# Layer 0's experts: TensorE's products in one fixed order, quarter-array products in two blocks an expert

## The chip, the cores and the metric

The kernel runs on one core of one Trainium2 chip. The metric is the device time of one execution in microseconds (us); the time before is 2729.64 us, the median of 3 runs (2728.22 to 2730.44). One execution under the profiler took 2732.13 us, with a span of 2730.4 us from its first to its last recorded instruction. TensorE multiplies (PE), VectorE and ScalarE (DVE, ACT) do the elementwise work, GpSimd (POOL) adds and issues the indirect transfers, SyncE (SP) issues the others.

## The reference

A block of two layers works on 1024 latent rows and 256 context rows of width 1024, in fp32. In each layer three token mixers (neighbourhood attention, a gated linear recurrence, a short convolution) are followed by 16 experts with expert choice: each expert takes its best rows, 128 latent rows and, in layer 0 alone, 32 context rows. Cut to what the change touches:

```python
def _expert_choice_ffn(h, w_router, w_gate, w_up, w_down):
    cap = EC_CAPACITY_FACTOR * t // N_EXPERTS          # 128 of 1024 latent rows, 32 of 256 context rows
    vals, idx = lax.top_k(aff.transpose(0, 2, 1), cap)
    xg = jax.vmap(lambda hb, ib: hb[ib])(h, idx)
    hid = silu(einsum('becd,edf->becf', xg, w_gate)) * einsum('becd,edf->becf', xg, w_up)
    out = einsum('becf,efd->becd', hid, w_down) * vals[..., None]
    return zeros.at[ib.reshape(-1)].add(ob.reshape(-1, d))

x  = x  + m_lat[5] * _expert_choice_ffn(h2,  w_router[l], w_exp_gate[l], w_exp_up[l], w_exp_down[l])
if need_ctx:                                           # layer 0 only
    cx = cx + m_ctx[5] * _expert_choice_ffn(hc2, w_router[l], w_exp_gate[l], w_exp_up[l], w_exp_down[l])
```

`w_exp_gate` and `w_exp_up` are 1024 x 512 per expert, `w_exp_down` is 512 x 1024.

## The kernel before, in words

`experts` (called once per layer) runs over the 16 experts. For each it does the following; the line is that of the code before.

- **Rows and weights.** `slots` turns the expert's column of ranks into row numbers with two small bf16 products per row tile (`slp`, L1148; the operand `O` is made on VectorE, L1144). `gather` (L1165) fetches 128 latent rows (`xg`) and the context's rows as quarters of a row (`xgc`) by indirect DMAs on GpSimd. `expert_w` (L1218) loads the weights as six tiles of 1 MB (`est`, two halves each of gate, up and down) on SyncE.
- **Transposing the rows** (`expert_x`). `xg` is transposed on TensorE in two halves of four 128 x 128 transposes (`xt`, L1231). Both halves go to the same PSUM bank, number 4 (`bank("xt")`, one buffer). For each half VectorE multiplies (`xm`, L1233, the only reader of the bank), GpSimd adds (L1234), ScalarE casts the high part (`xh`, L1235) and VectorE takes the rest (`xo`, L1236). The context's two transposes (`xtc`, L1244) go to bank 7, which the `slp` products share.
- **Gate and up** (`expert_up`). `split` makes of each weight half a high and a low part (`ewh` on ScalarE, L1178; `ewl` on VectorE, L1182) in three buffers. Per half 12 products (`pg`, L1280: high by high, rest by high, high by low) of the full array are accumulated over 128 latent rows. The context's products (`pgc`, L1265) take the fp32 weights as they are and use a quarter of the array's columns each (32 of 128), four side by side, into bank 5; four follow each weight half. `sc` copies them out.
- **The hidden layer** (`expert_hid`). `hid` (L1296, L1297) is transposed (`hidp`, L1300, bank 4) and copied (`hidT`, L1302). For the context four products sum the quarters (`hcp`, L1309, quarter array, bank 6); `hidc` and `upc` (L1312 to L1314) follow, two transposes on 64 rows (`hct`, L1317, bank 6), and `hcT` (L1319).
- **Down** (`expert_down`). Eight fp32 products for the latents (`pd`, L1335, banks 2 and 3) and eight on a quarter of the array for the context (`pdc`, L1341, bank 6), then `yo`, `yd`, `yc` (L1346 to L1352) and two indirect DMAs that add rows to the results (L1170).

Behind the last expert the modulation of layer 1 is computed (`adaln`: `aps`, L157, and `atp`, L171), the rows are loaded and normalised again, and the first projection of layer 1 (`pj`, L288) begins.

Within an engine the order of instructions is chosen by a scheduler from its own estimates of times; `issue_after` is the means by which the code can tie one instruction behind another. Before, TensorE's instructions of the experts have no such tie among themselves, and those of several steps lie among each other: an `xt` half stands between gate products, quarter-array groups stand between all others.

A plain fp32 product leaves two records in the trace: the eight `pd` of an expert are 16 records, and a group of four `pgc` is eight.

```python
ps = self.bank("xt" if need else "xt2", [P, 4, P], F32, "xt")      # need: layer 0; bank 4 alone
for j in range(4):
    nc.tensor.transpose(ps[:, j], xg[:, (k + j) * P:(k + j + 1) * P], self.idf)
xm = ep.tile([P, 4, P], F32, name="xm", bufs=2)
nc.vector.tensor_tensor(xm, ps, ...)
```

Of the kernel before, what the change touches and what calls it, by code (L numbers as in the profile page):

```python
# [19 lines left out]
P = 128  # L20
# [22 lines left out]
class Kern:  # L43
# [1177 lines left out]
    def expert_x(self, l, r, ep, eng=None):  # L1221
# [16 lines left out]
        if need:  # L1238
# [4 lines left out]
            for c in range(2):  # L1243
                nc.tensor.transpose(ps[:, c], xgc[:, c * P:(c + 1) * P], self.idf)  # L1244
# [5 lines left out]

    def expert_up(self, l, r, ep, first=False):
# [4 lines left out]
        pc, sc = None, []  # L1256

        def ctx_mm(gu, hf, st):

            nonlocal pc  # L1260
            if hf == 0:
                pc = self.bank("upc", [P, 512], F32, "pgc")
            for k in range(4):
                kk = 4 * hf + k
                nc.tensor.matmul(pc[32 * k:32 * k + 32], r["xc"][:, kk % 2, 32 * (kk // 2):32 * (kk // 2) + 32],  # L1265
                                 st[:, 512 * k:512 * k + 512], start=hf == 0, stop=hf == 1, tile_position=(0, 32 * k),
                                 skip_group_check=True)
            if hf == 1:
                t = ep.tile([P, 512], F32, name=f"sc{gu}", bufs=1)
                nc.scalar.copy(t, pc)  # L1270
                sc.append(t)
        late = []
        for gu in range(2):
            n = 0
            for hf in range(2):
                st = r[("gate", "up")[gu]][hf]
                wh, wl = r["pre"].pop(0) if r.get("pre") else self.split(self.ws, st, [P, 2048], "ew", 3)
# [5 lines left out]
                if need:  # L1283
                    late.append((gu, hf, st))
                    if len(late) > 1 * first:
                        ctx_mm(*late.pop(0))
        for x in late:
            ctx_mm(*x)
        return acc, sc

    def expert_hid(self, l, r, up, ep):
        nc = self.nc
        need = l < DEPTH - 1
        (pg, pu), sc = up
        hid = ep.tile([P, 512], F32, name="hid", bufs=1 + need)
        nc.scalar.activation(hid, pg, AF.Silu)  # L1296
        nc.vector.tensor_tensor(hid, hid, pu, ALU.mult)  # L1297
        ps = self.bank("xt" if need else "downc", [P, 4, P], F32, "hidp")
        for j in range(4):
            nc.tensor.transpose(ps[:, j], hid[:, j * P:(j + 1) * P], self.idf)  # L1300
        hT = ep.tile([P, 4, P], F32, name="hidT", bufs=2)
        nc.scalar.copy(hT, ps)  # L1302
        if need:

            ps = self.bank("downc", [P, 256], F32, "hcp")
# [5 lines left out]
            hc, uc = [ep.tile([64, 256], F32, name=n, bufs=1) for n in ("hidc", "upc")]  # L1311
            nc.scalar.activation(hc, ps[:64], AF.Silu)  # L1312
            nc.vector.tensor_copy(uc, ps[64:])
            nc.vector.tensor_tensor(hc, hc, uc, ALU.mult)  # L1314
            ps = self.bank("downc", [P, 2, 64], F32, "hct")
            for c in range(2):
                nc.tensor.transpose(ps[:, c], hc[:, P * c:P * c + P], self.idf[:64, :64])  # L1317
            hcT = ep.tile([P, 2, 2, 32], F32, name="hcT", bufs=2)
            nc.vector.tensor_copy(hcT.rearrange("p h c s -> p c h s"), ps.rearrange("p c (h s) -> p c h s", h=2))  # L1319
        return hT, (hcT if need else None)  # L1320

    def expert_down(self, l, r, hid, ep, g5, g5c, xl, xc):
# [6 lines left out]
        for hf in range(2):  # L1329
            st = r["down"][hf]  # L1330

            for k in range(2):
                for nn in range(2):
                    c = 1024 * k + 512 * nn
                    self.downed = nc.tensor.matmul(po[nn], hT[:, 2 * hf + k], st[:, c:c + 512],  # L1335
                                                   start=hf == 0 and k == 0, stop=hf == 1 and k == 1)
            for k in range(2):
                if need:
                    for nn in range(2):
                        o = 64 * k + 32 * nn  # L1340
                        nc.tensor.matmul(pd[o:o + 32], hcT[:, hf, k], st[:, 1024 * k + 512 * nn:1024 * k + 512 * nn + 512],  # L1341
                                         start=hf == 0, stop=hf == 1, tile_position=(0, o), skip_group_check=True)
# [12 lines left out]
    def experts(self, l, xl, xc):  # L1355

        nc = self.nc
        with self.pool(f"ex{l}") as ep, self.pool(f"ws{l}") as self.ws, self.pool(f"ew3_{l}") as ew3:
# [12 lines left out]
            self.nw = 0  # L1371

# [18 lines left out]
            start(2, rs[0]["xd"])  # L1391
            for e in range(NE):
# [146 lines left out]
```

## Time and profile before

| | |
|---|---|
| median of 3 runs | 2729.64 us (2728.22 to 2730.44) |
| profiled execution | 2732.13 us |
| its span | 2730.4 us, 55190 instructions |
| PE busy | 2504.4 us (92%) |
| DVE busy | 1884.3 us (69%) |
| ACT busy | 1131.4 us (41%) |
| POOL busy | 669.3 us (25%) |
| chain that ended last | PE 67%, DVE 18%, DMA 5%, issue 4%, ACT 3% |
| in it: `pg` / `pd` / `pgc` | 13% / 8% / 2% |
| DMA | 507.12 MB, mean 186 GB/s |

The profiled execution lies 2.5 us above the median and 1.7 us above its span. A busy share is a mean over the whole program, whose stages differ: layer 0's experts lie between about 1005 and 1458 us, and what bounds them must be read there, not from the shares. The chain is followed backwards from the last instruction to whatever released each one; a step that stands in it was late there in this execution.

### The profile page before, as it was taken

The numbers are of one execution on the slowest core, as the hardware profiler recorded it, in microseconds if no ns is written. First come the engines' busy times: TensorE is split into PE (matmuls) and PEld (weight loads), VectorE is DVE, ScalarE is ACT, GpSimd is POOL, SyncE is SP. The second block draws the span as 40 slices with busy tenths as digits, with TensorE's granted clock in tenths as the row PEclk, the third lists the DMA queues.
The fourth block names the chain that finished last, engine by engine and source line by source line (L and its number), as shares of the span: only waits on it lengthen the run. The fifth ranks groups of instructions, "written<-read, shape, count | busy, mean of one in ns | idle before, by whom it ended". The sixth has DMA issues, their size and how long they took to land.

```text
span 2730.4 us, 55190 instructions
## 1 busy us (share of the span) xinstructions
PE 2504.4 (92%) x21959; PEld 1906.9 (70%) x21959; DVE 1884.3 (69%) x4046; ACT 1131.4 (41%) x1878; POOL 669.3 (25%) x621
## 2 busy tenths in 40 slices
PE   7999999998999979999996999999958899589997
PEld 4998887894677855555554988778844677367664
DVE  4258887857666586777754368787858874787874
ACT  4224433324554534444434334333314554345452
POOL 1000000035444633333311000000045532222241
PEclk9999999998999979999998999999979999789999
DMA  7332324247354948888887332423176355889994
GB/s 281 102 108 71 114 68 123 66 138 243 113 160 135 349 151 278 281 280 279 283 280 212 94 105 74 124 84 89 49 200 225 94 163 183 300 281 370 377 376 127
DMA packets 347936, 507.12 MB, mean 186 GB/s; under 512 B 53380, under 2 KB 203072, under 8 KB 346592
## 3 DMA queue, kind: packets, MB, share of 16 engines
q1 hardware_dynamic: 336416, 465.85, 50.4%
q0 software_dynamic: 11264, 37.75, 5.9%
q8 instruction: 173, 2.83, 0.4%
q14 instruction: 83, 0.68, 0.1%
HBM read 410.10 MB, written 94.90 MB: 185 GB/s over the span
## 4 chain that ended last, share of the span: by engine, by line
PE 67%; DVE 18%; DMA 5%; issue 4%; ACT 3%; POOL 2%; SPq 1%; POOLq 0%; DVEq 0%; ACTq 0%
PE pg L1280 13%; PE pj L277 12%; PE pd L1335 8%; PE pj L288 8%; PE po L828 6%; PE nao L786 3%; PE pgc L1265 2%; PE npt L762 2%; PE sA L733 1%; DVE Kt L375 1%; PE aps L157 1%; DVE Kt L376 1%; DVE Qt L378 1%; PE hl L365 1%; PE xt L1231 1%
## 5 line engine op out<-in xcount | busy, mean ns | idle before, releaser
L1182 DVE TENSOR_TENSOR ewl<-est,ewh 128x2048 fp32r<-128x2048 f32 x126 | 298.1, 2371 | 109.7 <-ACT ewh L1178 108.6
L1178 ACT CAST ewh<-est 128x2048 fp32r<-128x2048 f32 x128 | 243.4, 1905 | 170.9 <-PE pg L1280 130.5
L277 PE MATMUL pj<-hl,whi 128*128 128x320 f32 (+2 forms) x912 | 310.2, 340 | 0.0
L277 PE MATMUL pj<-hh,whi 128*128 128x320 f32 (+2 forms) x912 | 309.9, 340 | 0.0
L277 PE MATMUL pj<-hh,wlo 128*128 128x320 f32 (+2 forms) x912 | 308.7, 339 | 0.0
L288 PE MATMUL pj<-whi,hh 128*128 128x256 f32 x960 | 277.8, 290 | 4.5 <-ACT nev L566 4.1
L288 PE MATMUL pj<-whi,hl 128*128 128x256 f32 x960 | 276.8, 291 | 0.8 <-DVE hl L239 0.8
L288 PE MATMUL pj<-wlo,hh 128*128 128x256 f32 x960 | 275.5, 288 | 0.0
L1335 PE MATMUL pd<-est,hidT 128*128 128x512 f32 x512 | 232.2, 596 | 2.1 <-ACT hidT L1302 2.1
L288 PEld LDWEIGHTS pj<-whi,hh 128*128 128x128 f32 x960 | 186.0, 194 | 8.8 <-ACT nev L566 5.2
L288 PEld LDWEIGHTS pj<-wlo,hh 128*128 128x128 f32 x960 | 185.9, 194 | 2.2 <-issue 1.3
L288 PEld LDWEIGHTS pj<-whi,hl 128*128 128x128 f32 x960 | 184.6, 194 | 3.5 <-issue 1.3
L277 PEld LDWEIGHTS pj<-hh,whi 128*128 128x128 f32 x912 | 172.2, 189 | 13.7 <-issue 0.9
L277 PEld LDWEIGHTS pj<-hl,whi 128*128 128x128 f32 x912 | 172.2, 189 | 13.5 <-issue 1.9
L277 PEld LDWEIGHTS pj<-hh,wlo 128*128 128x128 f32 x912 | 172.1, 189 | 13.0 <-issue 1.1
L1335 PEld LDWEIGHTS pd<-est,hidT 128*128 128x128 f32 x512 | 95.2, 189 | 110.7 <-issue 103.3
L265 DVE TENSOR_TENSOR wlo<-wst,whi 128x1024 fp32r<-128x1024 f32 (+1 forms) x72 | 75.2, 1058 | 131.7 <-ACT whi L264 130.6
L1280 PE MATMUL pg<-ewh,xh 128*128 128x512 f32 x512 | 156.8, 424 | 3.1 <-ACT xh L1235 3.0
L752 POOL TENSOR_SCALAR S<-S,sm 128x768 f32<-128x768 f32 (+2 forms) x108 | 108.6, 1007 | 188.3 <-DVE sm L751 166.8
L1280 PE MATMUL pg<-ewl,xh 128*128 128x512 f32 x512 | 147.7, 404 | 0.0
L1280 PE MATMUL pg<-ewh,xo 128*128 128x512 f32 x512 | 142.3, 398 | 2.1 <-DVE xo L1236 2.1
L750 ACT ACTIVATE S<-S,mn 128x768 f32<-128x768 f32 (+2 forms) x108 | 98.6, 913 | 85.2 <-DVE mn L745 79.6
(369 smaller groups left out, 5560.9 us busy)
## 6 DMA issues: line engine op xcount, KB each, us to landing
est<-in_w_exp_gate_dram SPq DMA_DIRECT2D x64, 1024.0 KB
est<-in_w_exp_up_dram SPq DMA_DIRECT2D x64, 1024.0 KB
est<-in_w_exp_down_dram SPq DMA_DIRECT2D x64, 1024.0 KB
wm<-in_w_mod_dram SPq DMA_DIRECT2D x80, 512.0 KB
wst<-in_w_in_dram SPq DMA_DIRECT2D x88, 256.0 KB
pna<-nev SPq DMA_DIRECT2D x180, 64.0 KB
wos<-in_w_out_dram SPq DMA_DIRECT2D x42, 256.0 KB
mst<-mix SPq DMA_DIRECT2D x32, 320.0 KB
```

The costliest lines, as they stand in the source:

```text
L265: nc.vector.tensor_tensor(b, c, a, ALU.subtract)
L277: nc.tensor.matmul(ps[:, :cn], sel(a(k)), b[:, k, c0:c0 + cn], start=n == 0, stop=n == 3 * KD - 1)
L288: nc.tensor.matmul(ps[:, :2 * P], b[:, k, t * P:(t + 1) * P], a(k).rearrange("p a n -> p (a n)"), start=n == 0, stop=n == 3 * KD - 1)
L750: nc.scalar.activation(S[:, :w], S[:, :w], AF.Exp, scale=-1.0, bias=mn[:, 1:2], accum_out=sm[:, 0:1])
L752: nc.gpsimd.tensor_scalar(S[:, :w], S[:, :w], sm[:, 1:2], 1.0, ALU.mult, ALU.mult)
L762: nc.tensor.transpose(pt[:kn, i], S[:, c:c + kn], self.idf)
L786: nc.tensor.matmul(po[64 * X:64 * X + 64, gi], V[:kn, tt, 64 * X:64 * X + 64], PT[X][:kn, i], start=i == 0, stop=i == len(ch) - 1, tile_po ...
L828: nc.tensor.matmul(ps, a, b, start=n == 0, stop=n == len(ops) - 1)
L1178: nc.scalar.copy(hi, src)
L1182: nc.vector.tensor_tensor(lo[:, :m], src[:, :m], hi[:, :m], ALU.subtract)
L1280: nc.tensor.matmul(acc[gu], a[:, 4 * hf + k], b[:, 512 * k:512 * k + 512], start=n == 0, stop=n == 3 * KD - 1)
L1335: self.downed = nc.tensor.matmul(po[nn], hT[:, 2 * hf + k], st[:, c:c + 512], start=hf == 0 and k == 0, stop=hf == 1 and k == 1)
```

## The change

All of it concerns the experts of layer 0 (`need`); layer 1 keeps its order.

- A new helper `then` ties each TensorE product or transpose inside it behind the one before it (`self.pel`). In layer 0 all of `expert_x`, `expert_up`, `expert_hid`, `expert_ctx`, `expert_ctx_hid` and `expert_down` runs under it, so that their order on TensorE is that of the code. The `slp` products of `slots` stay untied.
- The context's gate and up products (`ctx_mm`) are put together: 16 in a row between the latent's gate and up products (behind both for the first expert), into banks 5 and 6.
- `hcp` moves directly behind the up products and ahead of `pdc` of the expert before it, so that these two also form one block. `hcp` and `hct` use bank 5 in place of 6.
- `hct` transposes 128 rows of `hidc` (64 of them filled before; now `hidc` has 128 rows and ScalarE fills all), and `hcT` reads the first 64 columns.
- `expert_x` of the expert after next is called between `pdc` and `pd` (`mid`), both of its halves directly behind each other.

```diff
         for k in range(0, KD, 4):
             ps = self.bank("xt" if need else "xt2", [P, 4, P], F32, "xt")
             for j in range(4):
-                nc.tensor.transpose(ps[:, j], xg[:, (k + j) * P:(k + j + 1) * P], self.idf)
+                with self.then(need):
+                    nc.tensor.transpose(ps[:, j], xg[:, (k + j) * P:(k + j + 1) * P], self.idf)
...
+    def then(self, on=True):
...
+        def after(f):
+            def g(*a, **k):
+                with tc.issue_after(self.pel.ins) if self.pel is not None else nullcontext():
+                    self.pel = f(*a, **k)
+                return self.pel
+            return g
+        nc.tensor.matmul, nc.tensor.transpose = after(mm), after(tr)
...
+        with self.then(need):
+            prods(0)
+            if need and not first:
+                ctx_mm(0)
+                ctx_mm(1)
+            prods(1)
+            if need and first:
+                ctx_mm(0)
+                ctx_mm(1)
         return acc, sc
...
+    def expert_ctx(self, sc):
+
+        nc = self.nc
+        ps = self.bank("upc", [P, 256], F32, "hcp")
+        with self.then():
             for i, t in enumerate(sc):
                 for h in range(2):
                     o = 64 * i + 32 * h
                     nc.tensor.matmul(ps[o:o + 32], self.sel, t[:, 256 * h:256 * h + 256], start=True, stop=True,
                                      tile_position=(0, o), skip_group_check=True)
...
+        hc, uc = ep.tile([P, 256], F32, name="hidc", bufs=1), ep.tile([64, 256], F32, name="upc", bufs=1)
+        nc.scalar.activation(hc, ps, AF.Silu)
+        nc.vector.tensor_copy(uc, ps[64:])
+        nc.vector.tensor_tensor(hc[:64], hc[:64], uc, ALU.mult)
+        pt = self.bank("upc", [P, 2, P], F32, "hct")
+        with self.then():
             for c in range(2):
-                nc.tensor.transpose(ps[:, c], hc[:, P * c:P * c + P], self.idf[:64, :64])
...
+                nc.tensor.transpose(pt[:, c], hc[:, P * c:P * c + P], self.idf)
...
         if need:
             pd = self.bank("downc", [P, 512], F32, "pdc")
+            with self.then():
...
+            if mid:
+                mid()
         po = [self.bank("down", [P, 512], F32, "pd") for _ in range(2)]
...
             for e in range(NE):
                 if e + 3 <= NE:
                     start(e + 3, rs[e + 1]["xd"])
-                hid = self.expert_hid(l, rs[e], up, ep)
-                if e + 2 < NE:
+                if not need and e + 2 < NE:
                     self.expert_x(l, rs[e + 2], self.xp)
                 if e + 1 < NE:
                     up = self.expert_up(l, rs[e + 1], ep)
-                self.expert_down(l, rs[e], hid, ep, g5, g5c, xl, xc)
+                    if need:
+                        pc = self.expert_ctx(up[1])
+                more = lambda: self.expert_x(l, rs[e + 2], self.xp) if e + 2 < NE else None
+                self.expert_down(l, rs[e], (hid, hidc if need else None), ep, g5, g5c, xl, xc, more)
+                if e + 1 < NE:
+                    hid = self.expert_hid(l, rs[e + 1], up, ep)
+                    if need:
+                        hidc = self.expert_ctx_hid(pc, ep)
```

How this moves the instructions is shown for TensorE and VectorE. A row is the line, the operation, the result and its operands, the tile's shape and how many follow each other; after the change every tied TensorE instruction has the line of the helper's caller (L1265).

TensorE in a middle expert before, from a quarter-array group among the gate products on:

```order
L1231 MATMUL xt<-idf,xg 128x128 x3
L1309 MATMUL hcp<-sc_13529,sel 32x256 x2
L1309 MATMUL hcp<-sc_13572,sel 32x256 x2
L1231 MATMUL xt<-idf,xg 128x128
L1244 MATMUL xtc<-idf,xgc 128x128 x2
L1280 MATMUL pg<-ewl,xh 128x512 x3
L1280 MATMUL pg<-ewh,xh 128x512 x4
L1280 MATMUL pg<-ewh,xo 128x512 x4
L1280 MATMUL pg<-ewl,xh 128x512 x4
L1335 MATMUL pd<-est,hidT 128x512 x5
L1265 MATMUL pgc<-est,xct 32x512 x8
L1335 MATMUL pd<-est,hidT 128x512 x3
```

After the change, the block of context products of one expert:

```order
L1265 MATMUL pgc<-est,xct 32x512 x5
L1148 LDWEIGHTS O
L1148 MATMUL slp<-pay,O 128x5
L1148 LDWEIGHTS O
L1148 MATMUL slp<-pay,O 128x5
L1265 MATMUL pgc<-est,xct 32x512 x11
```

The two `slp` rows stand inside the block, which is so in 12 of the 16 experts. From the last up products on to the next expert's gate products:

```order
L1265 MATMUL pg<-ewl,xh 128x512 x4
L1265 MATMUL hcp<-sc_13929,sel 32x256 x2
L1265 MATMUL hcp<-sc_13940,sel 32x256 x2
L1265 MATMUL pdc<-est,hcT 32x512 x8
L1265 MATMUL xt<-idf,xg 128x128 x8
L1265 MATMUL xtc<-idf,xgc 128x128 x2
L1265 MATMUL pd<-est,hidT 128x512 x8
L1265 MATMUL hidp<-idf,hid 128x128 x4
L1265 MATMUL hct<-idf,hidc 128x128 x2
```

Here the two halves of `xt`, formerly between gate and up products, stand directly behind each other and behind `pdc`, and the quarter-array instructions stand in one block of `pgc` and one of `hcp` with `pdc`.

VectorE in a middle expert before, around the two `xm` that read the halves:

```order
L1233 TENSOR_TENSOR xm<-xt,A_12256 128x512
L1351 TENSOR_TENSOR yd<-pdc,yd 64x512
L1352 SCALAR_TENSOR_TENSOR yc<-yd,val,g5c 64x512
L1160 TENSOR_REDUCE val<-slp 128x1
L1182 TENSOR_TENSOR ewl<-est,ewh 128x2048
L1236 TENSOR_TENSOR xo<-xm,xh 128x512
L1233 TENSOR_TENSOR xm<-xt,A_12256 128x512
L1247 TENSOR_TENSOR xct<-xtc,A_12256 128x256
L1182 TENSOR_TENSOR ewl<-est,ewh 128x2048
L1248 TENSOR_TENSOR xct<-xct,mt_93 128x256
L1313 COPY upc<-hcp 64x256
```

After the change:

```order
L1182 TENSOR_TENSOR ewl<-est,ewh 128x2048
L1349 TENSOR_TENSOR hid<-hid,pg 128x512
L1182 TENSOR_TENSOR ewl<-est,ewh 128x2048
L1333 COPY upc<-hcp 64x256
L1234 TENSOR_TENSOR xm<-xt,A_12256 128x512
L1391 TENSOR_TENSOR yd<-pdc,yd 64x512
L1334 TENSOR_TENSOR hidc<-hidc,upc 64x256
L1392 SCALAR_TENSOR_TENSOR yc<-yd,val,g5c 64x512
L1234 TENSOR_TENSOR xm<-xt,A_12256 128x512
L1249 TENSOR_TENSOR xct<-xtc,A_12256 128x256
L1237 TENSOR_TENSOR xo<-xm,xh 128x512
```

Now `hid`, an `ewl` (of the following expert's first up half) and `upc` stand ahead of the first `xm`, and three small instructions on the context between the two `xm`.

TensorE at the start of layer 0's experts before, behind the first expert's own transposes:

```order
L1231 MATMUL xt<-idf,xg 128x128 x8
L1148 LDWEIGHTS O
L1148 MATMUL slp<-pay,O 128x5
L1148 LDWEIGHTS O
L1148 MATMUL slp<-pay,O 128x5
L1280 MATMUL pg<-ewh,xh 128x512 x8
```

After the change:

```order
L1148 MATMUL slp<-pay,O 128x5
L1265 MATMUL xtc<-idf,xgc 128x128 x2
L1265 MATMUL xt<-idf,xg 128x128 x8
L1265 MATMUL xtc<-idf,xgc 128x128 x2
L1265 MATMUL pg<-ewh,xh 128x512 x4
L1265 MATMUL pg<-ewh,xo 128x512 x4
```

Before, the first products follow the first expert's transposes; now the transposes of the first two experts, latent and context, stand ahead of them.

## Rows read from the trace of the kernel before

**Rows 1.** Windows view, layer 0's experts: stretch, busy (count) per engine, clock, DMA

```profile
1028.00:1352.00 324.00, 324.00 (x1751) 176.31 (x1744) 240.03 (x317) 140.62 (x144) 111.51 (x72) 1.00 0.84 282
```

**Rows 2.** Timeline, TensorE, one expert: start, us, line, out<-in, shapes, count

```profile
1166.64 1.07 PE L1280 MATMUL pg<-ewl,xh 128*128 128x512 f32 x4
1167.64 1.06 PE L1265 MATMUL pgc<-est,xct 128*32 128x512 f32 x8
1168.64 0.96 PE L1280 MATMUL pg<-ewh,xh 128*128 128x512 f32 x3
...
1171.45 0.64 PE L1231 MATMUL xt<-idf,xg 128*128 128x128 f32 x4
1171.84 0.48 PE L1280 MATMUL pg<-ewh,xh 128*128 128x512 f32 x1
...
1177.67 0.64 PE L1309 MATMUL hcp<-sc,sel 128*32 128x256 f32 x8
1178.24 0.33 PE L1231 MATMUL xt<-idf,xg 128*128 128x128 f32 x1
...
1181.18 1.07 PE L1280 MATMUL pg<-ewl,xh 128*128 128x512 f32 x4
1182.09 4.45 PE L1335 MATMUL pd<-est,hidT 128*128 128x512 f32 x10
1186.47 1.92 PE L1265 MATMUL pgc<-est,xct 128*32 128x512 f32 x16
1188.32 2.84 PE L1335 MATMUL pd<-est,hidT 128*128 128x512 f32 x6
```

**Rows 3.** Timeline, TensorE, a group of 16 cut in two

```profile
1401.52 1.92 PE L1265 MATMUL pgc<-est,xct 128*32 128x512 f32 x14
1403.36 0.33 PE L1317 MATMUL hct<-idf,hidc 64*128 64x64 f32 x2
1403.63 1.04 PE L1265 MATMUL pgc<-est,xct 128*32 128x512 f32 x2
1404.60 6.28 PE L1335 MATMUL pd<-est,hidT 128*128 128x512 f32 x14
```

**Rows 4.** Timeline, ScalarE, cast of the next expert's weights

```profile
1181.38 1.91 ACT L1178 CAST ewh<-est 128x2048 fp32r<-128x2048 f32 x1 [0.23 <-PE pg L1280]
```

**Rows 5.** Timeline, VectorE, the same expert

```profile
1175.52 2.29 DVE L1182 TENSOR_TENSOR ewl<-est,ewh 128x2048 fp32r<-128x2048 f32 x1
...
1183.01 0.43 DVE L1313 COPY upc<-hcp 64x256 f32<-64x256 f32 x1
1183.36 0.68 DVE L1236 TENSOR_TENSOR xo<-xm,xh 128x512 fp32r<-128x512 f32 x1
```

**Rows 6.** Timeline, TensorE, start of layer 0's experts

```profile
1002.08 1.12 PE L1231 MATMUL xt<-idf,xg 128*128 128x128 f32 x4 [0.78 <-DVE xm L1233]
...
1005.67 3.75 PE L1280 MATMUL pg<-ewh,xh 128*128 128x512 f32 x8
...
1026.10 0.60 PE L1300 MATMUL hidp<-idf,hid 128*128 128x128 f32 x4
```

**Rows 7.** Timeline, GpSimd, second expert's latent gather

```profile
1012.51 1.69 POOL L1165 DMA_INDIRECT xg<-h2l,ix  x1 [0.30 <-DVE xo L1236]
```

**Rows 8.** View of tile xgc from 985 to 1060: landing of gathers

```profile
DMA to landing us min/median/max: 4.6/6.2/6.5
```

**Rows 9.** Timeline, all engines, from layer 0's experts to layer 1's projection

```profile
1448.65 4.49 PE L157 MATMUL aps<-est,sT 128*32 128x512 f32 x40
...
1455.89 1.90 PE L1341 MATMUL pdc<-est,hcT 128*32 128x512 f32 x16
...
1478.96 0.29 PEld L288 LDWEIGHTS pj<-whi,hh 128*128 128x128 f32 x1 [0.64 <-issue]
```

**Rows 10.** Windows view, a pause of TensorE and the stretch behind

```profile
495.60:497.40 1.80, 0.18 (x19) 0.13 (x16) 1.74 (x5) 0.72 (x2) 0.00 (x0) 1.00 0.74 187
497.40:502.00 4.60, 4.60 (x62) 4.56 (x62) 4.35 (x13) 0.85 (x2) 0.00 (x0) 0.63 0.17 48
```

More of the change, by code (lines that the diff above doesn't have):

```diff
@@ L1 @@
-from contextlib import ExitStack, nullcontext
+from contextlib import ExitStack, contextmanager, nullcontext
 import math
@@ L1242, in expert_x @@
             ps = self.bank("small", [P, 2, P], F32, "xtc")
-            for c in range(2):
-                nc.tensor.transpose(ps[:, c], xgc[:, c * P:(c + 1) * P], self.idf)
+            with self.then():
+                for c in range(2):
+                    nc.tensor.transpose(ps[:, c], xgc[:, c * P:(c + 1) * P], self.idf)
             v = lambda t: t.rearrange("p c (i s) -> p c i s", i=4)
@@ L1255, in expert_up, with prods @@
         acc = [self.bank("up", [P, 512], F32, "pg") for _ in range(2)]
[L1256 to L1273, printed above, removed]
+        sc = []
+        def prods(gu):
             n = 0
             for hf in range(2):
-                st = r[("gate", "up")[gu]][hf]
-                wh, wl = r["pre"].pop(0) if r.get("pre") else self.split(self.ws, st, [P, 2048], "ew", 3)
+                wh, wl = r["pre"].pop(0) if r.get("pre") else self.split(self.ws, r[("gate", "up")[gu]][hf], [P, 2048],
+                                                                         "ew", 3)
                 for a, b in ((xh, wh), (xo, wh), (xh, wl)):
@@ L1282, in expert_up, with ctx_mm @@
                         n += 1
[L1283 to L1288, printed above, removed]
+        def ctx_mm(gu):
+            pc = self.bank(("upc", "downc")[gu], [P, 512], F32, "pgc")
+            for hf in range(2):
+                st = r[("gate", "up")[gu]][hf]
+                for k in range(4):
+                    kk = 4 * hf + k
+                    nc.tensor.matmul(pc[32 * k:32 * k + 32], r["xc"][:, kk % 2, 32 * (kk // 2):32 * (kk // 2) + 32],
+                                     st[:, 512 * k:512 * k + 512], start=hf == 0, stop=hf == 1, tile_position=(0, 32 * k),
+                                     skip_group_check=True)
+            t = ep.tile([P, 512], F32, name=f"sc{gu}", bufs=1)
+            nc.scalar.copy(t, pc)
+            sc.append(t)
+        with self.then(need):
[7 more added lines that the diff above has]
+                ctx_mm(1)
         return acc, sc
-    def expert_hid(self, l, r, up, ep):
+    def expert_ctx(self, sc):
         nc = self.nc
[L1293 to L1305, printed above, removed]
+        ps = self.bank("upc", [P, 256], F32, "hcp")
+        with self.then():
             for i, t in enumerate(sc):
@@ L1310, in expert_hid, with expert_ctx_hid, expert_down @@
                                      tile_position=(0, o), skip_group_check=True)
[L1311 to L1315, printed above, removed]
-            for c in range(2):
-                nc.tensor.transpose(ps[:, c], hc[:, P * c:P * c + P], self.idf[:64, :64])
[L1318 to L1322, printed above, removed]
+        return ps
+    def expert_ctx_hid(self, ps, ep):
+        nc = self.nc
[5 more added lines that the diff above has]
+        with self.then():
+            for c in range(2):
+                nc.tensor.transpose(pt[:, c], hc[:, P * c:P * c + P], self.idf)
+        hcT = ep.tile([P, 2, 2, 32], F32, name="hcT", bufs=2)
+        nc.vector.tensor_copy(hcT.rearrange("p h c s -> p c h s"), pt[:, :, :64].rearrange("p c (h s) -> p c h s", h=2))
+        return hcT
+    def expert_hid(self, l, r, up, ep):
+        nc = self.nc
+        need = l < DEPTH - 1
+        (pg, pu), _ = up
+        hid = ep.tile([P, 512], F32, name="hid", bufs=1 + need)
+        nc.scalar.activation(hid, pg, AF.Silu)
+        nc.vector.tensor_tensor(hid, hid, pu, ALU.mult)
+        ps = self.bank("xt" if need else "downc", [P, 4, P], F32, "hidp")
+        with self.then(need):
+            for j in range(4):
+                nc.tensor.transpose(ps[:, j], hid[:, j * P:(j + 1) * P], self.idf)
+        hT = ep.tile([P, 4, P], F32, name="hidT", bufs=2)
+        nc.scalar.copy(hT, ps)
+        return hT
+    def expert_down(self, l, r, hid, ep, g5, g5c, xl, xc, mid=None):
         nc = self.nc
@@ L1391, in experts @@
             start(2, rs[0]["xd"])
+            hid = self.expert_hid(l, rs[0], up, ep)
+            if need:
+                pc = self.expert_ctx(up[1])
+                hidc = self.expert_ctx_hid(pc, ep)
             for e in range(NE):
```

41 lines of the change are left out of this document (29 added, 12 removed).

## The prediction, before the run

> **What bounds the kernel now.** I read the page first (PE is busy 92% of the span and leads the chain of waits), then the windows view of the stage that the change touches, then the timelines of its engines, and last the seams at either end of the stage. The windows view shows 324.00 us of PE work in a stretch of 324.00 at granted clock 1.00, with VectorE busy for 240.03 of it and GpSimd for 111.51 [rows 1]. So in the middle of layer 0's experts TensorE never waits: what the change takes from TensorE's work is gained in full, and every wait that it puts into TensorE's order is lost in full. That is the first thing to see. The second is why there is no wait: after half an `xt`, gate products follow at once [rows 2], so that VectorE has time to empty bank 4 before the second half needs it. The third is that the stage has seams. Before the first products TensorE waits for rows, and behind the last one it waits for the context's results to go to memory and come back [rows 6, 9].
>
> **Fewer quarter-array groups.** Eight `pgc` records take 1.00 (1167.64 to 1168.64), sixteen 1.85 (1186.47 to 1188.32) [rows 2]: 0.15 for a group and 0.85 for each eight. The four products ahead of such a group take 1.00 (1166.64 to 1167.64) where the same four ahead of `pd` take 0.91 (1181.18 to 1182.09) [rows 2], so entering costs 0.09 more, and a group costs 0.24 in all. Before, an expert has five groups (three of `pgc`, `hcp`, `pdc`); after, one of `pgc` and one of `hcp` with `pdc`. That saves 3 x 0.24 = 0.72. `hct` on 128 rows costs what two full transposes cost: four take 0.39 (1171.45 to 1171.84) [rows 2], two 0.20, against 0.27 on 64 rows (1403.36 to 1403.63) [rows 3]: 0.07 less. So an undisturbed expert gains 0.79.
>
> **The cut.** In 12 experts two untied `slp` stand inside the block of `pgc`. The nearest rows are a group of 16 that was cut by `hct`: 14 records 1.84, the cutting pair 0.27, the last two 0.97 [rows 3], where sixteen whole take 1.85. The cut thus costs 1.84 + 0.97 - 1.85 = 0.96, and 0.09 to enter again: 1.05. An expert with a cut loses 1.05 - 0.79 = 0.26, one without gains 0.79: 12 x 0.26 - 4 x 0.79 = 0.0. The bounds are a plain group's 0.24 for the cut, which makes this 12 x 0.81 less, -9.8, and 1.05.
>
> The Trainium skill (TensorEngine Tiling (Array Packing), section Tiling Modes) says "Mode switching requires drain". By that alone a cut would be no more than one more change of mode, and the term would be the -9.8; the cut group in the trace shows more, and I go by the trace.
>
> **The two halves of `xt`.** This is the main term. Both halves use bank 4, so the second waits until VectorE's `xm` has read the first. Take the end of the last up product as zero (1182.09 [rows 2]). TensorE then does `hcp` (1177.67 to 1178.24 for its eight records, 0.57 [rows 2]) and `pdc` without a new entry (1.70), and 0.09 for entering: the first half starts at 2.36, ends at 2.75, and the second would follow there. VectorE's order, though, has ahead of `xm`: an `ewl` of the next gate half, `hid`, an `ewl` of the next first up half, `upc`. That up half needs the weight buffer which the last up products use, so its cast starts only with the last four products: the same cast started at 1181.38, 0.71 ahead of zero, and took 1.91 [rows 4], to 1.20. Its `ewl` can't start before, and the `ewl` and `hid` ahead of it end later: the former at about 0.76, and `hid` at 1.37 (128x512 elements, 0.68 as `xo`, less the 0.08 by which instructions overlap, as the 0.43 that is followed after 0.35 shows [rows 5]). Then come `ewl` with 2.29 less 0.08 [rows 5], to about 3.58, `upc` with 0.35, to 3.93, and `xm` with the same 0.68 as `xo` [rows 5], to some 4.6. The second half starts at 4.6 rather than 2.75: TensorE stands for **1.85**. Two halves are made inside an expert 14 times (for the third to the sixteenth), so 14 x 1.85 = **26 us**. The bounds: 0.78, which TensorE waited for `xm` at the start where VectorE was free [rows 6], or 11 us; and 2.7, if the buffer comes free only with the last of the four products, 0.91 later, or 37 us. I take 1.85, since the cast before did start 0.71 before the end of the last product.
>
> What stands behind `xt` is covered: `xtc`, then the 16 records of `pd` with ten in 4.38 (1182.09 to 1186.47 [rows 2]), 7 us, in which GpSimd's addition, ScalarE's cast and `xo` of the next but one expert, `hid` for `hidp` and `upc` and `hidc` for `hct` have their time. If that cover went, `hidp` would wait for `hid`, which by the sum above ends at 1.4, long before. The DMAs of the weights keep their order; with PE slower they have more slack, and I cost them at nothing.
>
> **The start.** Before, the first product stands at 1005.67, behind the first expert's transposes. After, the second expert's `xt` and `xtc` stand ahead of it. The gathers of that expert are issued by GpSimd at 1012.51 for 1.69 [rows 7], then `xgc`; gathers land 4.6 to 6.5 us after issue [rows 8]. From 1012.51 + 1.69 and the median 6.2 follows 1020.4, and with the transposes 1021 for the first product. The first expert's 48 products take 48 x 0.23 (four in 0.91) = 10.9, and a stretch behind a pause loses some 1.7 (4.60 us at clock 0.63 after 1.80 with PE busy for 0.18 [rows 10]): 1033.6, where the first expert's `hidp` stood at 1026.10 [rows 6]. That is 7.5 later. The waits of the following two experts for their slots, since `slp` and `xtc` share bank 7, I put at 2.5 more, an estimate (two waits of some 1.3, midway between the 0.78 and the 1.80 of [rows 6, 10]): **+10**, bounds 4 (half of the gathers' delay made up) and 16.
>
> **The end.** `hct`, `hcT` and `pdc` of the last expert follow each other with only a copy between: +0.5. Then there is a gain. Before, `pdc` is last (1455.89 + 1.90) and layer 1's first projection loads at 1478.96 [rows 9], 21.2 later, for the context's rows go to memory and come back. After, `pdc` stands ahead of `pd` (7 us) and of all 64 `aps` records (40 in 4.49 [rows 9], so 7.2), and the way of the context's rows starts 14.2 earlier against the end of TensorE's work. If it alone counted, 14.2 would be won; but the latents' rows and the modulation, from `aps` itself, are ready later than that. I take **-11**, bounds 0 and -14.
>
> **Sum.** 0 + 26 + 10 + 0.5 - 11 = +25.5. The profiled execution took 2732.1, 2.5 over the median; with 2757.6 for it, the median is **2755**. Layer 1's experts are not changed.
>
> **The rivals.**
>
> *The pauses also slow the clock.* Before, 1.80 us with TensorE hardly busy were followed by a stretch at a mean of 0.63 [rows 10], between the levels of 1.2 and 2.4 GHz, which loses 4.60 x 0.37 = 1.7 us. If each of the 14 pauses did so, 14 x 1.7 = 24 more: 2779. Against it: at the 0.78 pause of the start [rows 6] nothing of the kind follows, and TensorE was busy for longer around these pauses.
>
> *The cut costs only a drain.* With 0.24 for it rather than 1.05, 9.8 less: 2745. For it speaks that five `pgc` and eleven are long groups, where the expensive remainder [rows 3] had two; against it, that the remainder's 0.97 is longer than eight records of a whole group, whatever their number. The sentence of the Trainium skill quoted above (TensorEngine Tiling (Array Packing), section Tiling Modes) would make this the case; no row before shows so long a block cut.
>
> *The pause is mostly hidden.* If VectorE reaches `xm` soon (the `ewl` of the up half done early because the buffer came free early), 14 x 0.5 = 7 remain; with 10 and -11 and a cut between the bounds (-3), the total is +3.5: 2733.
>
> *Faster.* The order on VectorE decides by one place: if the first `xm` is read before 2.75, there is no pause at all. Then the sum is -9.8 (the cut at a plain group's price) + 0 + 10 + 0.5 - 11 = -10.3, so 2719. For that `xm` would have to start by 2.07, `upc` by 1.72 and the `ewl` of the up half by -0.5, so that its cast would have to end there; the cast row ends at 1.20 after the same zero [rows 4]. So I give this little.
>
> *The change doesn't do what it says.* The tie is only on order, and the order shown above has it in every expert; `slp` is not tied and already breaks the block in 12 of 16. That is in the sum.
>
> **How the numbers follow.** A measurement of this kernel tells a difference of 0.2%, or 5.5 us: the same is 2724 to 2735. The forecast has a chance of 0.68 (from 2738, with the pause at its lower bound and a little off the start, to 2772, with both at their upper), the slow clock 0.10, the cheap cut 0.07 (2745, inside the forecast's range), a hidden pause 0.08, and no pause 0.07. Slower are these first three, 0.85; the same 0.08; faster 0.07. The forecast is the likeliest's 2755. The range leaves out the last two and half of the slow clock: 2738 to 2776, which takes in the pause from 1.0 to 2.7.
>
> **What would show it.** Right: in the changed profile TensorE stands for 1.5 to 2.2 us ahead of the second half of `xt` in each middle expert, released by VectorE's `xm`; the period of an expert grows by about 2; the first product stands at about 1021; the records of `pgc` come in two pieces with a second piece longer by about 1 than its count; from the end of PE's experts to the first projection 10 us rather than 21. Wrong: a middle stretch with no idle time on PE (then the pause isn't there), a granted clock below 1.00 in it (the first rival), a wait at `hidp` or at the first gate product of an expert (then VectorE or ScalarE is the bound), or a `slp` that waits for its `O` inside the block, which I cost at nothing since `O` is made an expert earlier.

## The result

The changed kernel takes 2780.47 us, the median of 4 runs (2777.31 to 2784.70), against 2730.04 of the kernel before (2728.22 to 2737.03, 4 runs): a ratio of 1.0174, 95% interval 1.0157 to 1.0190. That is 50 us slower. The prediction had the sign, forecast 25 us, and its range ended at 2776. A second set of runs of the same kernel gave 2775.06 (ratio 1.0170, 1.0147 to 1.0194).

The page of its profile, in two places: the span and the engines' busy time, and the granted clock in 40 slices.

```profile
span 2780.7 us, 55155 instructions
...
PE 2524.2 (91%) x21959; PEld 1931.1 (69%) x21959; DVE 1893.1 (68%) x4046; ACT 1133.2 (41%) x1878; POOL 636.5 (23%) x621
...
PEclk9999999998999969999999999999989999789999
```

TensorE is busy for 2524.2 us where it was 2504.4, with as many instructions, so a part of the loss is slower work, not waiting. The windows view of the changed kernel in the stretch of [rows 1], and then four windows around two of its pauses (columns: stretch, length, busy time and count of PE, PEld, DVE, ACT and POOL, granted clock, DMA share, GB/s):

```profile
1028.00:1352.00 324.00, 304.71 (x1588) 174.02 (x1587) 223.91 (x282) 133.37 (x132) 75.33 (x63) 0.97 0.77 249
...
1092.41:1096.71 4.30, 2.50 (x25) 0.81 (x17) 4.24 (x6) 1.52 (x3) 0.00 (x0) 1.00 0.95 378
...
1098.00:1101.00 3.00, 3.00 (x5) 1.33 (x4) 3.00 (x5) 0.49 (x1) 1.94 (x2) 0.50 0.00 0
...
1247.04:1251.32 4.28, 2.49 (x24) 0.81 (x16) 4.22 (x6) 1.52 (x3) 0.00 (x0) 1.00 0.95 363
1251.32:1259.00 7.68, 7.68 (x23) 3.81 (x24) 7.68 (x10) 1.24 (x2) 3.61 (x3) 1.00 0.37 77
```

TensorE no longer works through: 304.71 of 324.00. The pause that ends at 1096.71 is followed by a stretch at granted clock 0.50, the level of 1.2 GHz; the like pause that ends at 1251.32 is followed by none. Summed over windows of 0.5 us, each such stretch costs 1.71 us.

TensorE's timeline of one expert of the changed kernel (start, us, engine, line, operation, result and operands, shapes, count, idle time before):

```profile
1174.37 1.90 PE L1265 MATMUL pgc<-est,xct 128*32 128x512 f32 x10
1176.21 0.20 PE L1148 MATMUL slp<-pay,O 128*128 128x5 bf16 x2
1176.34 2.78 PE L1265 MATMUL pgc<-est,xct 128*32 128x512 f32 x22
1179.05 1.20 PE L1265 MATMUL pg<-ewh,xh 128*128 128x512 f32 x4
...
1184.72 0.64 PE L1265 MATMUL hcp<-sc,sel 128*32 128x256 f32 x8
1185.17 1.90 PE L1265 MATMUL pdc<-est,hcT 128*32 128x512 f32 x16
1187.01 0.66 PE L1265 MATMUL xt<-idf,xg 128*128 128x128 f32 x4
1189.47 0.83 PE L1265 MATMUL xt<-idf,xg 128*128 128x128 f32 x4 [1.81 <-DVE xm L1234]
1190.09 0.63 PE L1265 MATMUL xtc<-idf,xgc 128*128 128x128 f32 x2
1190.51 8.38 PE L1265 MATMUL pd<-est,hidT 128*128 128x512 f32 x16
```

and VectorE's at the same place:

```profile
1185.35 0.68 DVE L1349 TENSOR_TENSOR hid<-hid,pg 128x512 f32<-128x512 f32 x1
1185.95 2.28 DVE L1182 TENSOR_TENSOR ewl<-est,ewh 128x2048 fp32r<-128x2048 f32 x1
1188.26 0.43 DVE L1333 COPY upc<-hcp 64x256 f32<-64x256 f32 x1
1188.72 0.69 DVE L1234 TENSOR_TENSOR xm<-xt,A 128x512 f32<-128x512 f32 x1
```

The chain of the prediction stands there link by link: `hid`, the `ewl` of the up half, `upc`, `xm`, and 1.81 us of waiting (1.85 was forecast). All 14 pauses are 1.79 to 1.81. Seven of the 14 are followed by a low stretch; the last row of TensorE's timeline is one of them (`pd` with 8.38, where the same 16 records take 7.03 at full clock).

The start and the end, on TensorE:

```profile
1018.78 0.66 PE L1265 MATMUL xtc<-idf,xgc 128*128 128x128 f32 x2 [2.74 <-DMA xgc<-h2c,ix]
1022.60 1.11 PE L1265 MATMUL xt<-idf,xg 128*128 128x128 f32 x4 [3.16 <-DMA xg<-h2l,ix]
...
1025.70 2.05 PE L1265 MATMUL pg<-ewh,xh 128*128 128x512 f32 x4
...
1038.70 3.64 PE L1265 MATMUL pgc<-est,xct 128*32 128x512 f32 x32
...
1042.41 0.64 PE L1265 MATMUL hidp<-idf,hid 128*128 128x128 f32 x4
...
1491.33 1.92 PE L1265 MATMUL pdc<-est,hcT 128*32 128x512 f32 x16 [0.43 <-ACT hidT L1355]
1493.19 7.13 PE L1265 MATMUL pd<-est,hidT 128*128 128x512 f32 x16
1500.25 7.07 PE L157 MATMUL aps<-est,sT 128*32 128x512 f32 x64
...
1520.73 0.80 PE L288 MATMUL pj<-whi,hh 128*128 128x256 f32 x2 [1.28 <-DMA x<-x]
```

The first product waits for the second expert's gathers, as forecast, and the last `pdc` stands ahead of `pd` and of the modulation, whose 64 `aps` end at 1507.3; from there to the first projection it is 13.4 us, where 21.2 passed before [rows 9].

I cut both profiles at the first expert's first `xt`, at the last `hidp` and at the first projection of layer 1. Ahead of the first cut the changed kernel is 4.6 us later (1004.84 against 1000.22), between the first two it takes 485.2 us against 438.7, to the projection 30.7 against 40.1, and from there to the end 1260.0 against 1251.4: 4.6 + 46.6 - 9.4 + 8.6 = 50.3, the difference of the spans. The 46.6 are 14 pauses (25.2), seven low stretches behind them (12.0), and the start: at the second expert's `hidp` the changed kernel was 15.3 later since the first cut, 13.5 without the pause that lies ahead of it. The rest is -4.1. These last two belong together: some 2.3 of the 13.5 is no loss but work that now stands ahead of this mark and stood behind it before (`pdc` of the first expert and `hcp` of the second, which take 2.29 in the timeline above, 1184.72 to 1187.01). So the start costs 11.2, and the rest is -1.8.

So two amounts were not in the forecast: the low clock with 12.0, and 13.2 outside of the experts, where no line of the code was changed. The experiments went after these two, beside the pause.

### The profile page after: what moved, and what is told of

The parts are those of the page before. It is cut to its first block, busy times and chain, and to the rows that moved or that the text cites. A ratio compares the mean times of both kernels' runs of the same rounds, so it can differ in the third digit from the quotient of the medians.

```text
span 2780.7 us, 55155 instructions
## 1 busy us (share of the span) xinstructions
PE 2524.2 (91%) x21959; PEld 1931.1 (69%) x21959; DVE 1893.1 (68%) x4046; ACT 1133.2 (41%) x1878; POOL 636.5 (23%) x621
## 4 chain that ended last, share of the span: by engine, by line
PE 54%; DVE 13%; DMA 4%; ACT 2%; issue 2%; POOL 2%; SPq 1%; POOLq 0%; DVEq 0%; ACTq 0%
PE pg L1288 6%; PE po L828 6%; PE pj L277 6%; PE pj L288 5%; PE pg L1265 5%; PE pd L1265 4%; PE pd L1381 4%; PE nao L786 3%; PE pgc L1265 2%; DVE ewl L1182 2%; PE npt L762 2%; PE aps L157 2%; PE sA L733 1%; ACT ewh L1178 1%; DVE mg L1020 1%
## 5 line engine op out<-in xcount | busy, mean ns | idle before, releaser
L1235 POOL TENSOR_TENSOR xm<-xm,mt 128x512 f32<-128x512 f32 x60 | 80.7, 1355 | 209.3 <-DVE xm L1234 195.1
L1265 PE MATMUL pd<-est,hidT 128*128 128x512 f32 x256 | 123.2, 638 | 0.0
L157 PE MATMUL aps<-wm,sT 128*32 128x512 f32 x320 | 83.6, 668 | 40.1 <-DMA wm<-in_w_mod_dram 40.1
L786 PE MATMUL nao<-PT,nav 128*64 128x128 f32 (+1 forms) x1296 | 113.8, 282 | 6.4 <-ACT PT L765 4.8
L1381 PE MATMUL pd<-est,hidT 128*128 128x512 f32 x256 | 115.1, 592 | 0.7 <-ACT hidT L1355 0.7
```

The costliest lines, as they stand in the source:

```text
L157: nc.tensor.matmul(ps[32 * j:32 * j + 32], self.sT[:, k, :], w[j], start=k == 0, stop=k == KD - 1, tile_position=(0, 32 * j))
L786: nc.tensor.matmul(po[64 * X:64 * X + 64, gi], V[:kn, tt, 64 * X:64 * X + 64], PT[X][:kn, i], start=i == 0, stop=i == len(ch) - 1, tile_po ...
L1265: self.pel = f(*a, **k)
L1381: self.downed = nc.tensor.matmul(po[nn], hT[:, 2 * hf + k], r["down"][hf][:, c:c + 512], start=hf == 0 and k == 0, stop=hf == 1 and k == 1)
```

## The experiments

### The changed kernel again

> The changed kernel as it is, a second time, to see what of its 50 us repeats. Theory: the 14 pauses of 1.80 us ahead of the second half of xt repeat exactly, so does the late start, and the time is 2780 +-4. In the first profile 4.8 us were lost before layer 0's experts and 8.6 behind the first projection of layer 1, where the order of the instructions is (nearly) the same; there and in the experts TensorE's clock fell to 1.2 GHz for stretches that cost 1.71 us each. If these stretches fall by chance, their number differs here and the two amounts with them; if they belong to the program, the same stretches are there again.

Measured: 2775.06 us (2773.46 to 2784.78), a little below the range expected. The pauses are 1.80 again, 14 of them. Five are followed by a low stretch, not seven, and at other experts. The first `xt` stands at 998.76, 1.5 ahead of the kernel before, so the 4.6 ahead of the experts were chance. The time from the first projection to the end is 1262.7, 11.3 above that of the kernel before, so this part was not shown to be chance.

### The halves of `xt` apart

```diff
+        po = [self.bank("down", [P, 512], F32, "pd") for _ in range(2)]
-            if mid:
-                mid()
+        if need and mid:
+            mid(lambda: half(0))
+        else:
+            half(0)
+        half(1)
...
         for k in range(0, KD, 4):
+            if k and gap:
+                gap()
```

Here `half` issues four of the eight `pd`, and `gap` is the first of them.

> The second half of xt stands behind the first four products of pd instead of directly behind the first half (and the slp then stand outside or at the edge of the blocks of pgc, by the scheduler). Theory (the pause is VectorE's distance to xm, and the low clock follows from the pause): 14 x 1.80 = 25 us of waiting gone, the seven stretches at 1.2 GHz behind the pauses gone (7 x 1.71 = 12), and the cut of the block gone (12 x 1.05 = 12.6): about 2730. Rival (the low clock comes from the long quarter-array blocks, not from the pause): the stretches stay, about 2743. Rival (VectorE is the bound, and the wait turns up elsewhere, at hidp or at the next gate product): the period of an expert stays above 28.5 us.

Measured: 2722.35 us (2720.28 to 2730.07), a ratio to the kernel before of 0.9967 (0.9955 to 0.9980), 8 us below the theory. The windows view of the middle of the experts, and TensorE's timeline:

```profile
1050.00:1440.00 390.00, 389.73 (x2147) 227.65 (x2145) 287.70 (x357) 172.92 (x175) 102.34 (x84) 1.00 0.89 292
```

```profile
1211.50 3.64 PE L1267 MATMUL pgc<-est,xct 128*32 128x512 f32 x32
...
1223.21 0.66 PE L1267 MATMUL xt<-idf,xg 128*128 128x128 f32 x4
1223.70 3.60 PE L1267 MATMUL pd<-est,hidT 128*128 128x512 f32 x8
1227.14 0.60 PE L1267 MATMUL xt<-idf,xg 128*128 128x128 f32 x4
```

No pause, clock 1.00, no low stretch between 1033 and the end of the experts, though the `pgc` stand in one block of 32 records: the blocks of quarter-array products do not bring the low clock. VectorE does not become the bound. The period of an expert is 26.2 us where it was 27.2 before the change: without the pause and the cut the regrouping saves 1.03 an expert (0.79 was forecast). This one edit makes the difference between a loss of 44 to 50 us and a gain of 8. Not all of it is the second half's place: 25 us are the pauses and 8.5 to 12 the low stretches, but some 13 (12 x 1.11, measured below) come from the `slp`, which the scheduler now leaves outside the blocks.

### One product between the halves

`gap` issues one product of `pd`; the rest is as in the changed kernel, the cut of the `pgc` block in 12 experts too.

> Only one product of pd (two records, 0.86 us) stands between the two halves of xt; VectorE's order and the cut of the pgc block stay as in the changed kernel. Theory (the second half waits for xm, whatever stands between): each of the 14 pauses is shorter by the 0.86, 0.94 in place of 1.80, so 12 us less. On the clock: if a low stretch follows a pause whatever its length, 5 to 7 of the 14 are still followed by one of 1.71 us, 2768 or 2766; if it needs the longer pause, none is, and the time is about 2757. Rival (the low clock has nothing to do with the pause): 5 to 7 stretches, and at other places.

Measured: 2746.39 us (2744.24 to 2748.18), ratio 1.0060 (1.0045 to 1.0076), so 11 us below what the theory had even without low stretches. Windows view and one pause of it:

```profile
1050.00:1440.00 390.00, 376.76 (x1992) 212.95 (x1989) 283.69 (x348) 164.93 (x165) 96.37 (x80) 1.00 0.82 269
```

```profile
1172.18 1.02 PE L1267 MATMUL pd<-est,hidT 128*128 128x512 f32 x2
1174.14 0.66 PE L1267 MATMUL xt<-idf,xg 128*128 128x128 f32 x4 [0.94 <-DVE xm L1236]
```

The pause is 0.94 to 0.95 in each expert, shorter by the product's 0.86, as the theory has it: VectorE's `xm` comes when it comes. Not one of the 14 is followed by a low stretch. Over all profiles of kernels with the long pause it was 28 of 70 (7, 5, 5 in the changed kernel, 6 and 5 in the two below), with the short one none of 28, without any pause none. From the third expert on a low stretch comes only behind the long pause, and behind which ones changes from run to run. The length of a single pause is not all that counts, though: at the second expert six of the profiles with the tied start have the same waits of 0.21, 0.82 and 0.21 us around small `slp` products, and in three of them a low stretch follows, in three none. What the theory missed here is the part from layer 1's projection on, 1252.3 as before the change, and 4.3 us ahead of the experts (the first `xt` at 1000.51 against 1004.84).

### The `slp` tied

```diff
+        with self.then(not self.last and e >= 3):
             for t in range(n):
                 nc.tensor.matmul(ps[:, :5], O[:, t], ...)
```

> The slp products of the experts from the fourth on are tied into TensorE's order, between hct and the next gate products, so that nothing cuts the block of pgc; the pauses stay. Theory (a cut costs about 1.05): the block of 32 records takes 3.6 us as in the experts without a cut, where it took 4.7, the period falls by 1.05 in the 12 experts, 2768. Rival (a cut costs only another group's entry, 0.24): 2777. Rival (slp then waits for its operand O, which VectorE makes late): a new wait at slp, and no gain.

Measured: 2775.72 us (2774.90 to 2783.04), as the changed kernel in the same set. Both readings hold in part:

```profile
1192.34 0.34 PE L1266 MATMUL slp<-pay,O 128*128 128x5 bf16 x8
1193.70 0.20 PE L1266 MATMUL slp<-pay,O 128*128 128x5 bf16 x2 [1.01 <-DVE val L1161]
...
1199.41 3.64 PE L1266 MATMUL pgc<-est,xct 128*32 128x512 f32 x32
1202.98 1.20 PE L1266 MATMUL pg<-ewh,xh 128*128 128x512 f32 x4
```

The whole block takes 3.57 (1199.41 to 1202.98), the cut one took 4.68 (1174.37 to 1179.05): a cut costs 1.11, forecast 1.05. Why it costs so much can be read from pieces of other lengths. With one product between the halves the scheduler cuts the block at another place:

```profile
1159.05 1.91 PE L1267 MATMUL pgc<-est,xct 128*32 128x512 f32 x12
1160.89 0.20 PE L1148 MATMUL slp<-pay,O 128*128 128x5 bf16 x2
1161.03 2.77 PE L1267 MATMUL pgc<-est,xct 128*32 128x512 f32 x20
1163.72 0.50 PE L1267 MATMUL pg<-ewh,xh 128*128 128x512 f32 x1
```

Here 12 and 20 records take 1.84 and 2.69, and in the changed kernel 10 and 22 records take the same 1.84 and 2.71. Before, 16 take 1.85 and 8 take 1.00 [rows 2], 14 take 1.84 and 2 take 0.97 [rows 3]. A piece thus takes 0.15 and 0.85 for each begun eight records, that is for each begun set of four products side by side. A cut inside a set makes five begun sets of four: 5 x 0.85, 2 x 0.15 and the 0.13 of the `slp` are 4.68, as measured. By this estimate a cut between two sets would cost only the 0.15 and the 0.13; no run has one.

But the tied `slp` wait 0.3 to 1.0 for VectorE to read the bank which they share, and the waits from the first product to the last `hidp` rise from 26.5 to 36.0 us. Most of what the cut gave back (12 x 1.11) went into these new waits.

### The start free

```diff
-            self.expert_x(l, rs[0], self.xp, nc.vector)
-            self.expert_x(l, rs[1], self.xp)
+            self.expert_x(l, rs[0], self.xp, nc.vector, tie=False)
+            self.expert_x(l, rs[1], self.xp, tie=False)
```

> The transposes of the first two experts' rows are not tied; the first gate products then stand behind the first expert's own transposes, as before the change. Theory: the first product starts some 15 us earlier than 1025.7 and the start's 13 us are gone: 2768. Rival (the first experts are held by their weights or slots, which come no earlier): the gain at the first product is lost again at the second expert, 2778 or more.

Measured: 2768.47 us (2765.08 to 2770.90), ratio 1.0134 (1.0117 to 1.0151). The first product comes 5.4 us behind the first `xt` rather than 20.9. More than half of these 15 is lost again at once:

```profile
1007.88 2.07 PE L1265 MATMUL pg<-ewh,xh 128*128 128x512 f32 x4
...
1033.80 0.62 PE L1265 MATMUL hcp<-sc,sel 128*32 128x256 f32 x4 [1.81 <-ACT sc L1303]
...
1036.14 0.38 PE L1148 MATMUL slp<-pay,O 128*128 128x5 bf16 x8 [1.57 <-DVE val L1160]
```

From the first `xt` to the last `hidp` it takes 476.1 us, 464.2 without its low stretches, where the changed kernel takes 471.5: the tie at the start costs 7.3 net. That the time meets the theory's 2768 is luck: against the changed kernel in the same set, 2775.06, the gain is 6.6 and not 13.

### Both edits

> Both edits together: the second half of xt stands behind the first four products of pd, and the first two experts' transposes are not tied. Theory (the late start costs some 7 us, as the stage was shorter by that with the free start alone, its low clock left out): 7 us less than with the halves apart alone, 2715, below the kernel before by 15. Rival (without the pauses the stage is bound elsewhere and the start is made up): 2722 as before this edit.

Measured: 2719.83 us (2713.89 to 2726.46, 6 runs), ratio 0.9958 (0.9944 to 0.9973): faster than the kernel before by 10, and not to be told from the halves apart alone (0.9955 to 0.9980). In the experts it does gain: 425.9 us from the first `xt` to the last `hidp`, 5.9 less. From layer 1's projection on its profile has 1264.4 against 1258.2. Neither the theory nor the rival: the start's gain is there and was given back later, in the one profile that each of the two kernels has; whether that is program or chance was not tried.

### Chance or program, from layer 1's projection on

The kernel before a second time:

> The kernel before, a second profile, to see what of its time from the first projection of layer 1 to the end (1251.4 us in its first profile; 1258.2 to 1262.7 in the five profiles of changed kernels) is chance. Theory (the scheduler orders layer 1's attention otherwise behind the change, and that costs 5 us or more): 1250 to 1254 again. Rival (the first profile met few stretches of low clock by chance): 1257 or more. In its experts there is no stretch of low clock, 27.2 us for each expert.

and three more profiles:

> A third profile of the kernel before, for the time from layer 1's first projection to the end: 1251.4 and 1251.0 so far. If that time belongs to the program (the order of its instructions in layer 1), it is 1250 to 1253 here; if it falls by chance, with the stretches of low clock that an execution meets, it may be anything from 1250 to 1263.

> A third profile of the changed kernel: 1260.0 and 1262.7 from layer 1's first projection to the end so far. If it belongs to the program, 1259 to 1264 here; if it falls by chance, it may lie near 1251 too. In the experts: 14 pauses of 1.80, and 4 to 8 stretches of low clock behind them, each of 1.71.

> The kernel with one product between the halves a second time: 1252.3 from layer 1's first projection to the end in the first profile, the only one of a changed kernel that lies near the kernel before. If that belongs to the program, 1251 to 1254 again; if to chance, more. In the experts again no stretch of low clock behind the 14 pauses of 0.95, if the length of the pause decides; some, if it was chance.

Measured, from the first projection to the end: the kernel before 1251.4, 1251.0, 1247.7 (the third lies below the range expected for it); the changed one 1260.0, 1262.7, 1260.9; one product between 1252.3, 1253.3. (Times of these single runs: 2730.01, 2729.97, 2773.39 and 2752.00.) No profile of the changed kernel comes near one of the kernel before, so the difference belongs to the program. In this part TensorE is busy for 1129.6 to 1134.4 us in the changed kernel and for 1122.3 to 1126.3 before, and idle for 128.3 to 130.4 against 124.7 to 126.4: more of the loss is slower work than waiting. The third profile of the changed kernel has five low stretches behind its 14 pauses, the second one of the short pause none behind a pause of the experts from the third on; one follows at the second expert.

The difference begins some 130 us behind the projection, in the mixers of layer 1, where the changed kernel falls back by 2.8 to 4.0 us at one place in all three profiles. The third one there, ScalarE and TensorE:

```profile
1641.49 0.63 ACT L501 ACTIVATE gt<-gt 128x512 f32<-128x512 f32 x1 [3.86 <-DMA gt<-g]
...
1646.13 0.55 PE L341 MATMUL hl<-Qt,kz 128*32 128x32 f32 x40 [1.56 <-DVE Qt L378]
...
1648.01 0.77 PE L341 MATMUL hl<-Qt,kz 128*32 128x32 f32 x40 [1.32 <-DVE Qt L378]
```

and the kernel before at the same work:

```profile
1607.23 0.63 ACT L501 ACTIVATE gt<-gt 128x512 f32<-128x512 f32 x1 [2.04 <-DMA gt<-g]
...
1613.75 0.55 PE L341 MATMUL hl<-Qt,kz 128*32 128x32 f32 x40 [0.40 <-DVE Qt L378]
```

ScalarE stands longer behind a load (`gt`, 3.86 against 2.04), its `kz` copies come later, VectorE's `Qt` behind them too, and TensorE waits 2.9 in place of 0.4; a low stretch of 1.71 follows at 1647. The order of the instructions is not the cause of this first part: between some 30 and 560 us behind the projection TensorE, VectorE, ScalarE, GpSimd and the DMAs that SyncE issues stand in the same order in both kernels. What differs is how long after the store of `g` the load of it is issued. SyncE's queue in the third profile of the changed kernel, and then in the first of the kernel before:

```profile
1634.75 0.34 SPq L423 DMA_DIRECT2D g<-pev  x1
1638.68 0.34 SPq L485 DMA_DIRECT2D gt<-g  x1
```

```profile
1601.79 0.34 SPq L423 DMA_DIRECT2D g<-pev  x1
1604.34 0.34 SPq L485 DMA_DIRECT2D gt<-g  x1
```

It is 3.6 to 4.2 us in the three profiles of the changed kernel and 2.5 to 2.6 in those of the kernel before; with the halves apart, where the order from 30 us behind the projection is also the same, it is 2.5. Why it takes longer is open. The rest is lost in layer 1's attention, 560 to 760 us behind the projection. There the order of the instructions is not the same: the scheduler places them by its estimates, which the changed experts have presumably moved. Whether the other order is the cause there, and which of the exchanged instructions costs what, was not tried.

## Why the prediction was wrong

- **The pause: right.** 14 x 1.80 = 25.2 for a forecast of 26, by the chain that was forecast, and gone when the second half moves. Cover by `pd` held: nothing waits at `hidp` or at an expert's first product.
- **Groups and the cut: right.** A middle expert without a low stretch takes 29.2, 27.2 and 1.8 and 0.2 more; the forecast was 0.26. The cut costs 1.11. The rival by which it costs only another group's entry falls for this cut: 1.11 is over four times the 0.24, because the cut splits a set of four, as the lengths of the pieces show. The remainder of two records [rows 3] from which the forecast took its price had been split off a set in the same way. The Trainium skill (TensorEngine Tiling (Array Packing), section Tiling Modes) says that a change of mode drains the engine, but gives no price, so the 1.11 neither bears it out nor speaks against it.
- **The start: right to some 1 us.** The first product came 20.9 behind the first `xt`; the forecast (1021) lies 20.8 behind it. The first `hidp` came 11.7 later and not 7.5: the sum went from the 48 products straight to it, though the change puts the first expert's 32 records of `pgc` (3.57) ahead of it. Before, they stood behind it, so that is work moved and no loss. The waits around bank 7 were put at 2.5; they are 1.24, with a low stretch of 1.71 behind them. Measured 11.2, the moved work left out, for 10.
- **The end: right to 1 us,** -9.4 for -11 and 0.5.
- **The clock: the step that failed first.** I gave the slow clock behind the pauses 0.10, since the 0.78 pause of the start was followed by nothing of the kind. The price of one stretch was right (1.7 against 1.71), but that pause could not show a fall. The clock was already low around it: the granted clock of the kernel before is 0.50 from 1000.22 to 1013.80 (the row below this list). It was also a shorter pause: the run with 0.95 has no low stretch either. A pause of 1.80 was only in [rows 10], and it was followed by one. I should have gone by that row, and by part of the pauses rather than all or none: 12.0 here, 8.5 in the changed kernel's other two profiles.
- **Layer 1: the step that failed second.** "Layer 1's experts are not changed" stood for all that follows, at a cost of nothing and with no bounds, and the section on the change says that layer 1 keeps its order. That holds for the code alone: in layer 1's attention the scheduled order is not the same. From the projection on the changed kernel takes 1260.0 to 1262.7, the kernel before 1247.7 to 1251.4. Of this 2.8 to 4.0 us arise where the order is the same, behind the store and load of `g`; the cause of both parts stays open.

```profile
1000.22:1013.80 13.58, 9.99 (x37) 7.11 (x35) 12.42 (x24) 2.55 (x3) 2.27 (x2) 0.50 0.18 58
```

Put together for the first profile: the forecast's 25.5, less 0.8 at the pauses, 1.2 more at the start and 1.1 at the end, 12.0 for the clock, 8.6 in layer 1, the chance 4.6 ahead of the experts and -1.8 for the rest of the experts make 50.4; the spans differ by 50.3. The -1.8 are the groups and the cuts, put at 0.0: twelve experts with a cut lose 0.2 each and four without gain 1.03.

## What to carry to other kernels

When an order is written out by hand, look for two uses of one PSUM bank that end up next to each other: the second waits for the reader's whole queue, and four products put between them took away 25 us of waiting and 8.5 to 12 us of slow clock here. A block of quarter-array products that is cut inside a set of four loses the time of a whole set (0.85 of the 1.11 here). Price a wait on TensorE with the clock behind it, by a row with a wait as long, not by a shorter one. And where a scheduler orders the rest of the program, a change in one stage can cost time in all stages behind it, even where their order stays: that term needs bounds, and not a nothing.

## What I had not expected

From the third expert on, the low stretch goes with the length of the pause so sharply (28 of 70 behind 1.80 us, none of 28 behind 0.95) that taking away half of a wait took away all of the clock's loss there. And of 14 pauses alike to 0.02 us, with TensorE busy for the same 2.5 of the 4.3 us ahead, some are followed by the stretch at 1.2 GHz and others not, at other experts in each execution.
